# Dealing queued work by cost, with heads' tiles dealt anew and S's split kept on VectorE

## The chip, the cores and the metric

The kernel runs on one core of a Trainium2 chip. The time is device microseconds of one execution, from its first to its last instruction with what lies around them; of several executions the median is given. A core has engines that run side by side and meet through semaphores: TensorE (PE, matmuls), VectorE (DVE), ScalarE (ACT), GpSimd (POOL), and SyncE (SP), which here issues transfers. Each engine works through its own instructions in the order in which the program was written down.

## The reference

One layer of a hybrid decoder is computed for 1024 prompt rows and 8 x 4 sample rows, width 1024, in float32:

```python
z = _rmsnorm(x, norm_mix_g)
p = z @ w_in                      # h, c, b | u, v | q | gate logits gA, gB, gM
...
conv_out, conv_a_state = _causal_dwconv3(a_c * a_h, conv_a_prev, conv_a_w)
y_a = a_b * conv_out
y_b = u * _spatial_gate(v_n, sg_w, sg_b)
y_m = _mem_attention(q, mem_k, mem_v)      # 4 heads of 256, 256 memory rows
g = jax.nn.sigmoid(g.astype(jnp.float32)).astype(x.dtype)
g_a, g_b, g_m = jnp.split(g, N_BRANCH, axis=-1)
x = x + (g_a * y_a + g_b * y_b + g_m * y_m) @ w_o
h = _rmsnorm(x, norm_ffn_g) @ w_up
hc, conv_f_state = _causal_dwconv3(h, conv_f_prev, conv_f_w)
hc = hc + conv_f_b
a, gt = jnp.split(hc, 2, axis=-1)
x = x + (jax.nn.silu(gt) * a) @ w_down
```

The prompt's attention reads one shared memory (256 rows); each of the 8 sample groups has a cached memory of its own. The updated caches are outputs too.

## The kernel before

All activations stand with channels on the partitions and the 1056 rows (T) side by side, in 8 tiles of 128 channels. A float32 product is made of three matmuls on rounded parts: a value is split into a high part (cast on ScalarE) and a low part (value less high part, mostly on VectorE), and `three` (L205 to L207) adds high x high, high x low and low x high. `zhi` and `zlo` hold the parts of the normalised input, later of `S`, the sum of the gated branches.

The stages in order of time: norm and v (to about 240 us), the main stage (244 to 686), the pair stage (691 to 1029), w_o, the up projection, the down projection (to the end).

**Main stage.** It makes u, gB, q and gM, tile by tile (`main`). A tile is 3 chunks of 352 rows, and a chunk is 24 matmuls into one of three PSUM buffers `mm`. A u chunk is evacuated by one VectorE instruction (L1077), a gB chunk by a sigmoid on ScalarE (L1072) and one product on VectorE (L1091), a gM chunk by a sigmoid and two VectorE instructions (L1099, L1100). The order of tiles is the list `plan`, in which `"u0"` means tiles 0 and 1 of u, `"B1"` tiles 2 and 3 of gB, and so on; each string is the work during which one head's attention is done, the first and the last string go without one.

**Queued work.** What the attention and other small steps issue is put as closures into a queue `aux`. Twice in a chunk (after 12 matmuls, and at its end; I call this a slot) `weave` takes items off the queue: `pace(n)` says that the queue is to be empty after n slots, and `weave` gives out the number of items that this asks for. `drain` gives out all that are left. An item is called when its turn comes, and its instructions then stand on every engine behind all that was written before.

**A head's items** (`att_items`): `rows` turns the sample rows' q and writes them to DRAM (L816); `fetch` loads cached keys and values; `fetch_q` loads q rows to all partitions (L825); 16 `product` items, four VectorE products each (L837), make the sample rows' scores, each followed by an item that is a load or nothing; `kv_load` and `kv_split` bring the prompt's keys and values of this head and split them (cast on ScalarE, low part at L955 on VectorE); `score(i)` makes 12 matmuls (L968 to L970) for 256 prompt rows, then a maximum (L973), exponentials (L976), and the normalised probabilities on VectorE (L980, L983); `turn_p(i)` transposes them (L995); `value(i)` multiplies with the values. Then come the sample rows' softmax, `parts` (splits of the cached values, L883 and L884) and `against` (their matmuls, L897).

**Pair stage.** The projections h, c, b and gA go in steps of a seven-product scheme on 2 x 2 blocks. `b_forms(s)` makes block differences of the input ahead of it: `whole` adds high and low part on GpSimd (L1133), `minus` subtracts blocks on VectorE (L1139), `parts` splits (L1145 ScalarE, L1146 VectorE). `b_sums` makes the weight sums on GpSimd (L1191 to L1193), `b_prepare` splits a weight block for one step (L1204 ScalarE, L1205 VectorE). A step's 24 matmuls go to one of three PSUM buffers `pair`, and VectorE or ScalarE evacuates them (L1264 to L1291). These buffers lie where `mm` lay. `ORDER = (1, 2, 6, 5, 7, 3, 4)` is the order of a pair's seven steps.

**End of the pair stage.** In the last pair `b_end` says what follows each step: `to_parts` splits finished tiles of `S` into `zhi` and `zlo` (L1348 ScalarE, L1349 VectorE or GpSimd), `x_back` reads the residual input back into `S`, `units_o` queues the loads of w_o, `split_unit` and `split_lows` split its tiles (L182, L184).

## Time and profile before

| what | value |
| --- | --- |
| median of 3 runs | 1886.79 us (1886.17 to 1886.82) |
| profiled execution | 1886.49 us |
| its span | 1884.8 us |
| mean granted TensorE clock | 0.981 |
| TensorE idle, waiting for keys' low part (L955) | 27.4 us in 3 waits |
| TensorE idle, 684 to 702 us | 7.45 us |
| TensorE idle, 1010 to 1041 us | 7.15 us |

In the views quoted below, a row of waits names the waiting line and what it waited for, then total us, times and longest. A row of the timeline gives start, duration, engine, line, operation, output and inputs, and in brackets the idle time ahead of it with what ended it. A row of windows gives, for each engine, busy time and number of instructions, then the granted clock (1.00 is full speed), the share of the transfer engines and GB/s.

### The profile page before, as it was taken

To read this page: it belongs to the slowest core of one execution; us is meant where nothing else is said; L and a number is where in the kernel's file an instruction comes from. 1 tells how busy PE (TensorE), PEld (TensorE's weight loads), DVE (VectorE), ACT (ScalarE), POOL (GpSimd) and SP (SyncE) were. 2 spreads that over 40 slices of the span, in tenths; PEclk is the share of its full clock that TensorE was granted. 3 is DMA by queue.
4 is the path that set the end of the run, shared out by engine and by line. 5 is a ranking of instruction groups with operands and counts; after the bars stand their busy time and mean duration, and the time that the engine had idled before them with its cause. 6 is when DMAs were issued, how large, how long until landed. Compare 5 with 4: busy or idle time off the path is not lost.

```text
span 1884.8 us, 32215 instructions
## 1 busy us (share of the span) xinstructions
PE 1803.8 (96%) x12960; PEld 1774.1 (94%) x12960; DVE 1303.6 (69%) x2246; ACT 694.2 (37%) x1133; POOL 489.8 (26%) x545
## 2 busy tenths in 40 slices
PE   9999999989897989999998999999999999999997
PEld 8988999989897889999998998899999999899997
DVE  5577665574838687676868578888988898655433
ACT  6654325223332332232233333433333333444332
POOL 2231100000000424233322223566656654100000
PEclk9999999999998989999998999999999999999999
DMA  8736252524334201111113730222222322776652
GB/s 265 209 106 204 78 191 79 164 82 147 105 101 138 70 13 56 46 57 57 46 48 97 203 91 29 85 76 87 79 75 70 92 75 90 227 244 227 201 164 89
DMA packets 250145, 215.11 MB, mean 114 GB/s; under 512 B 7941, under 2 KB 235437, under 8 KB 249997
## 3 DMA queue, kind: packets, MB, share of 16 engines
q1 hardware_dynamic: 243252, 203.81, 35.0%
q10 hardware_dynamic: 6745, 9.25, 1.4%
q8 instruction: 102, 1.67, 0.4%
q14 instruction: 46, 0.38, 0.1%
HBM read 183.22 MB, written 29.81 MB: 113 GB/s over the span
## 4 chain that ended last, share of the span: by engine, by line
PE 57%; DVE 17%; issue 10%; POOL 9%; ACT 3%; DMA 2%; ACTq 0%; SPq 0%; DVEq 0%; POOLq 0%
PE pair L206 11%; PE pair L207 11%; PE pair L205 11%; PE mm L205 5%; PE mm L207 5%; PE mm L206 5%; DVE fs L837 4%; POOL fs L1663 2%; DVE wl L184 2%; POOL S L1575 2%; DVE fs L1646 1%; POOL S L1574 1%; POOL ws L1596 1%; POOL S L1573 1%; DVE wh L1593 1%
## 5 line engine op out<-in xcount | busy, mean ns | idle before, releaser
L205 PE MATMUL pair<-zhi,wh 128*128 128x264 f32 (+1 forms) x1608 | 474.9, 295 | 15.3 <-ACT zhi L1348 6.0
L206 PE MATMUL pair<-zlo,wh 128*128 128x264 f32 (+1 forms) x1608 | 471.6, 293 | 1.9 <-DVE zlo L1349 1.2
L207 PE MATMUL pair<-zhi,wh 128*128 128x264 f32 x1216 | 347.4, 286 | 2.4 <-DVE wh L1205 2.4
L205 PE MATMUL pair<-fs,wh 128*128 128x264 f32 (+1 forms) x1124 | 330.9, 294 | 4.7 <-DVE fs L1687 4.1
L206 PE MATMUL pair<-fs,wh 128*128 128x264 f32 (+1 forms) x1124 | 327.7, 292 | 0.7 <-DVE fs L1460 0.7
L205 PEld LDWEIGHTS pair<-zhi,wh 128*128 128x128 f32 x1608 | 306.9, 191 | 20.0 <-ACT zhi L1348 6.4
L205 PE MATMUL mm<-zhi,wh 128*128 128x352 f32 x960 | 315.4, 329 | 0.3 <-ACT zhi L267 0.3
L206 PE MATMUL mm<-zlo,wh 128*128 128x352 f32 x960 | 312.0, 325 | 1.0 <-POOL zlo L278 1.0
L207 PE MATMUL mm<-zhi,wl 128*128 128x352 f32 x960 | 311.1, 324 | 0.2 <-DVE wl L184 0.2
L206 PEld LDWEIGHTS pair<-zlo,wh 128*128 128x128 f32 x1608 | 307.0, 191 | 2.7 <-DVE zlo L1349 1.5
L184 DVE TENSOR_TENSOR wl<-ws,wh 128x1024 fp32r<-128x1024 f32 (+1 forms) x151 | 187.4, 1243 | 163.4 <-ACT wh L182 162.8
L207 PE MATMUL pair<-fs,wh 128*128 128x264 f32 x904 | 256.2, 283 | 0.0
L207 PEld LDWEIGHTS pair<-zhi,wh 128*128 128x128 f32 x1216 | 231.1, 190 | 2.7 <-DVE wh L1205 2.7
L205 PEld LDWEIGHTS pair<-fs,wh 128*128 128x128 f32 x1124 | 212.1, 189 | 5.8 <-ACT fs L1629 4.0
L206 PEld LDWEIGHTS pair<-fs,wh 128*128 128x128 f32 x1124 | 212.2, 189 | 0.9 <-DVE fs L1460 0.9
L182 ACT CAST wh<-ws 128x1024 fp32r<-128x1024 f32 (+1 forms) x152 | 153.5, 1013 | 150.8 <-PE pair L206 94.3
L206 PEld LDWEIGHTS mm<-zlo,wh 128*128 128x128 f32 x960 | 181.8, 189 | 1.8 <-POOL zlo L278 1.5
L205 PEld LDWEIGHTS mm<-zhi,wh 128*128 128x128 f32 x960 | 182.3, 190 | 1.1 <-ACT zhi L267 0.6
L207 PEld LDWEIGHTS mm<-zhi,wl 128*128 128x128 f32 x960 | 181.8, 189 | 0.5 <-DVE wl L184 0.5
L207 PEld LDWEIGHTS pair<-fs,wh 128*128 128x128 f32 x904 | 170.4, 188 | 0.0
L1646 DVE SCALAR_TENSOR_TENSOR fs<-fs,vec,fs 128x1024 f32<-128x1024 f32 x88 | 132.9, 1510 | 0.0
L207 PE MATMUL pair<-zhi,wl 128*128 128x352 f32 (+1 forms) x392 | 123.9, 316 | 1.4 <-DVE wl L184 1.4
(323 smaller groups left out, 3179.7 us busy)
## 6 DMA issues: line engine op xcount, KB each, us to landing
ws<-in_w_in SPq DMA_DIRECT2D x88, 512.0 KB, 4.5
ws<-in_w_down SPq DMA_DIRECT2D x60, 512.0 KB, 4.6
fs<-q_d SPq DMA_DIRECT2D x32, 512.0 KB, 8.4
ws<-in_w_up SPq DMA_DIRECT2D x46, 256.0 KB, 3.9
act_d<-fs SPq DMA_DIRECT2D x22, 528.0 KB, 3.2
S<-in_w_up SPq DMA_DIRECT2D x42, 256.0 KB, 2.9
fs<-in_cache_mem_k SPq DMA_DIRECT2D x16, 512.0 KB
fs<-in_cache_mem_v SPq DMA_DIRECT2D x16, 512.0 KB, 3.5
```

Source lines behind the costliest of these rows:

```text
L182: nc.scalar.copy(out=hi, in_=t)
L184: lows.append(lambda: eng.tensor_tensor(out=lo, in0=t, in1=f32(hi), op=ALU.subtract))
L205: mmul(ps, lhsT=wh, rhs=xh, start=first, stop=False)
L206: mmul(ps, lhsT=wh, rhs=xl, start=False, stop=False)
L207: mmul(ps, lhsT=wl, rhs=xh, start=False, stop=last)
L837: nc.vector.tensor_tensor_reduce(out=att["qr"][:, :256], in0=q[:, i, :], in1=t[:, 2 * (bb % 2) + mt, :], scale=1.0, scalar=0.0, op0=ALU.mu ...
L1573: tt(out=s1, in0=a21, in1=a22, op=ALU.add)
L1574: tt(out=s2, in0=s1, in1=a11, op=ALU.subtract)
L1575: tt(out=a21, in0=a11, in1=a21, op=ALU.subtract)
L1593: nc.vector.tensor_tensor(out=lo, in0=a, in1=f32(hi), op=ALU.subtract)
L1646: nc.vector.scalar_tensor_tensor(out=o[:, :NP], in0=hb[:, k : k + NP], scalar=w, in1=o[:, :NP], op0=ALU.mult, op1=ALU.add)
L1663: nc.gpsimd.tensor_tensor(out=g[:, :T], in0=g[:, :T], in1=outs[j, 0][:, :T], op=ALU.mult)
```

## The change

It has three parts. Line numbers of the changed kernel are 8 higher from the weaving on (9 and 12 near the end of the pair stage and behind).

1. *Weaving.* Each item of a head has a cost: 2.2 for a product, 0.2 for the item after it, 1.4 for the keys' split, 0.8 for `parts`, 0.4 for the others; items without a cost count 1. `weave` shares out costs and no longer numbers. The plan is dealt anew, so that four heads have 46, 34, 34 and 34 slots (58, 34, 34 and 30 before). Keys' load and split come one group of products sooner.
2. *Forms and sums.* The first half's `b_forms` begin one gB tile earlier and have 12 slots, where they had 6. `b_sums(0)` goes behind three of the second half's forms, where it stood behind all of them, and that queue has 11 slots, where it had 12.
3. *End of the pair stage.* All of S's splits go to VectorE, in pieces of two tiles; `units_o` is called after step 6, where it was after step 2; the last steps are the same in another notation.

```diff
+    def cost(go):
+        return getattr(go, "cost", 1.0)
+
+    def at_cost(x, go):
+
+        go.cost = x
+        return go
+
     def weave():
         split_lows()
-        due[0] += len(aux) / slots_left[0]
+        due[0] += sum(cost(go) for go in aux) / slots_left[0]
         slots_left[0] = max(1, slots_left[0] - 1)
-        while aux and due[0] > 0.999:
-            due[0] -= 1
+        while aux and due[0] > cost(aux[0]) - 0.001:
+            due[0] -= cost(aux[0])
             aux.popleft()()
...
-    for names in ("q0", "u0 B0 u1 B1 q1", "M0 u2 q2", "M1 B2 q3", "M2 u3 B3", "M3"):
+    for names in ("q0", "u0 B0 u1 q1", "B1 M0 q2", "M1 u2 q3", "B2 M2 u3 B3", "M3"):
...
-            no = lambda: None
+            no, small_no = lambda: None, at_cost(0.2, lambda: None)
...
-                    items.append(product(bb, mt))
-                    items.append(fetch_q(bb + 2) if mt and bb + 2 < 8 else no)
+                    items.append(at_cost(2.2, product(bb, mt)))
+                    items.append(at_cost(0.2, fetch_q(bb + 2)) if mt and bb + 2 < 8 else small_no)
...
+                if bb == 4:
+                    items += [kv_load, started]
                 if bb == 5:
-                    items += [kv_load, started]
-                if bb == 6:
-                    items.append(kv_split)
+                    items.append(at_cost(1.4, kv_split))
...
-                items.append(parts(bb // 2, bb % 2))
+                items.append(at_cost(0.8, parts(bb // 2, bb % 2)))
...
-            return items
+            return [go if hasattr(go, "cost") else at_cost(0.4, go) for go in items]
...
-                pace(6 * len(seq) - 2 if h < 3 else 30)
+                pace(6 * len(seq) - 2 if h < 3 else 34)
...
-                if (n, f) == ("gB", 7):
+                if (n, f) == ("gB", 6):
                     drain()
                     aux.extend(b_forms(0))
-                    pace(6)
+                    pace(12)
                 if (n, f) == ("gM", 6):
-                    aux.extend([lambda: (b_load(0, 0), b_load(0, 1), b_load(1, 0))] + b_forms(1))
-                    aux.extend([lambda: b_sums(0)] + [b_prepare] * 4)
-                    pace(12)
+                    forms1 = b_forms(1)
+                    aux.extend([lambda: (b_load(0, 0), b_load(0, 1), b_load(1, 0))] + forms1[:3])
+                    aux.extend([lambda: b_sums(0)] + forms1[3:] + [b_prepare] * 4)
+                    pace(11)
...
-        def to_parts(fr, r, eng=nc.vector):
+        def to_parts(fr, r):
             nc.scalar.copy(out=zhi[:, fr, r], in_=S[:, fr, r])
-            eng.tensor_tensor(out=zlo[:, fr, r], in0=S[:, fr, r], in1=f32(zhi[:, fr, r]), op=ALU.subtract)
+            nc.vector.tensor_tensor(out=zlo[:, fr, r], in0=S[:, fr, r], in1=f32(zhi[:, fr, r]), op=ALU.subtract)
...
         b_end = {
-            1: [lambda: to_parts(slice(0, 4), left, nc.gpsimd)],
-            2: [units_o, lambda: to_parts(slice(4, 6), left, nc.gpsimd)],
-            6: [lambda: to_parts(slice(6, 7), left)],
-            5: [lambda: to_parts(slice(0, 4), right), lambda: x_back(slice(0, 4)), split_unit, split_lows],
-            7: [split_unit, split_lows],
-            3: [lambda: to_parts(slice(4, 6), right), lambda: x_back(slice(4, 6)), lambda: to_parts(slice(7, 8), right)],
+            1: [lambda: to_parts(slice(0, 2), left), lambda: to_parts(slice(2, 4), left)],
+            2: [lambda: to_parts(slice(4, 6), left)],
+            6: [units_o, lambda: to_parts(slice(6, 7), left)],
+            5: [lambda: to_parts(slice(0, 2), right), lambda: to_parts(slice(2, 4), right),
+                lambda: x_back(slice(0, 4)), o_split],
+            7: [o_split],
+            3: [lambda: to_parts(slice(4, 6), right), lambda: x_back(slice(4, 6)), lambda: to_parts(slice(7, 8), right),
+                last_add, lambda: to_parts(slice(6, 7), right)],
         }
```

How this moves instructions is shown at three places on VectorE. The first is head 1 from the keys' low part (L955, now L963) to the first maximum (L973, now L981); a product is a pair of ISA rows (L837, now L845), `sig` and `S` rows are gM evacuations. Before:

```order
L837 ISA fs_3766,sc<-fs_3997,fs_3971 128x256
L837 ISA sc 128x1
L955 TENSOR_TENSOR fs_4081<-fs_4041,fs_4080 128x1024
L837 ISA fs_3766,sc<-fs_4039,fs_3971 128x256
...
L1077 TENSOR_TENSOR S<-mm,S 128x352
...
L973 TENSOR_REDUCE mx_4131<-aux 128x2
L980 RECIPROCAL sm_4132<-sm_4132 128x2
```

Of the change:

```order
L1107 TENSOR_TENSOR sig<-sig,fs_2968 128x352
L1108 TENSOR_TENSOR S<-S,sig 128x352
L963 TENSOR_TENSOR fs_3922<-fs_3861,fs_3921 128x1024
L192 TENSOR_TENSOR wl<-ws,wh 128x1024
L845 ISA fs_3586,sc<-fs_3859,fs_3801 128x256
...
L1107 TENSOR_TENSOR sig<-sig,fs_2969 128x352
L1108 TENSOR_TENSOR S<-S,sig 128x352
...
L845 ISA fs_3586,sc<-fs_3903,fs_3801 128x256
...
L981 TENSOR_REDUCE mx_4031<-aux 128x2
L988 RECIPROCAL sm_4032<-sm_4032 128x2
```

Before, 56 of the 64 products stand ahead of the low part and 8 behind it, with one u evacuation; now 48 and 16, with a weight split and two gM evacuations. On TensorE 264 main matmuls stand between `rows` and the first score of heads 1 to 3 (204, 204 and 180 before), and 276 in head 0 (300 before); after them come two scores, then the first `turn_p` (before, in heads 1 and 2, 12 main matmuls between the two scores).

The second place is VectorE ahead of the first pair step: block differences, splits of them (into `fs`), gM evacuations, and weight splits (`wh`). Before:

```order
L1139 TENSOR_TENSOR fs_6647<-fs_6647,fs_6593 128x1056
L1146 TENSOR_TENSOR fs_6684<-fs_6647,fs_6683 128x1056
L1099 TENSOR_TENSOR sig<-sig,fs_5888 128x352
L1100 TENSOR_TENSOR S<-S,sig 128x352
L1205 TENSOR_TENSOR wh<-ws,wh 128x512 x2
L1099 TENSOR_TENSOR sig<-sig,fs_5888 128x352
L1100 TENSOR_TENSOR S<-S,sig 128x352
L1205 TENSOR_TENSOR wh<-fs_6716,wh 128x512 x2
```

Of the change:

```order
L1147 TENSOR_TENSOR fs_6651<-fs_6651,fs_6593 128x1056
L1154 TENSOR_TENSOR fs_6688<-fs_6651,fs_6687 128x1056
L1213 TENSOR_TENSOR wh<-ws,wh 128x512
L1107 TENSOR_TENSOR sig<-sig,fs_5721 128x352
L1108 TENSOR_TENSOR S<-S,sig 128x352
L1213 TENSOR_TENSOR wh<-ws,wh 128x512
L1213 TENSOR_TENSOR wh<-fs_6595,wh 128x512 x2
L1107 TENSOR_TENSOR sig<-sig,fs_5721 128x352
L1108 TENSOR_TENSOR S<-S,sig 128x352
```

The second half's differences stand at the same gM chunks as before; one weight split has moved ahead of the last-but-one gM evacuation, two more ahead of the last. On GpSimd the three sums stand ahead of the eighth `whole`, where they stood behind it.

The third place is VectorE at the end of the pair stage: weight splits (`wh`), evacuations of `pair`, and splits of `S`. Before:

```order
L1205 TENSOR_TENSOR wh<-ws,wh 128x512 x2
L1267 TENSOR_TENSOR sig<-pair,fs_6771 128x528
L1205 TENSOR_TENSOR wh<-ws,wh 128x512
L1279 TENSOR_TENSOR sig<-sig,fs_9903 128x528
L1280 TENSOR_TENSOR S<-S,sig 128x528
L1289 TENSOR_TENSOR fs_6771<-pair,fs_6771 128x528
L1349 TENSOR_TENSOR zlo<-S,zhi 128x528
L1289 TENSOR_TENSOR fs_6771<-pair,fs_6771 128x528
L1349 TENSOR_TENSOR zlo<-S,zhi 128x4x528
```

Of the change:

```order
L1213 TENSOR_TENSOR wh<-ws,wh 128x512
L1358 TENSOR_TENSOR zlo<-S,zhi 128x2x528 x2
L1213 TENSOR_TENSOR wh<-ws,wh 128x512
L1275 TENSOR_TENSOR sig<-pair,fs_6771 128x528
L1358 TENSOR_TENSOR zlo<-S,zhi 128x2x528
L1213 TENSOR_TENSOR wh<-ws,wh 128x512
L1287 TENSOR_TENSOR sig<-sig,fs_9903 128x528
L1288 TENSOR_TENSOR S<-S,sig 128x528
L1297 TENSOR_TENSOR fs_6771<-pair,fs_6771 128x528
L1358 TENSOR_TENSOR zlo<-S,zhi 128x528
L1297 TENSOR_TENSOR fs_6771<-pair,fs_6771 128x528
L1358 TENSOR_TENSOR zlo<-S,zhi 128x2x528 x2
```

Three splits of two tiles have come in between the weight splits and the evacuations; before they stood on GpSimd, as one of four tiles and one of two.

## The prediction

> **What bounds the kernel now.** The profiled execution took 1886.49 us, 0.3 us below the median of 1886.79; its span is 1884.8 us, so 1.7 us lie around it. The sum is made against 1886.5 and carried to the median as it is. First the page's busy shares:

> ```profile
> PE 1803.8 (96%) x12960; PEld 1774.1 (94%) x12960; DVE 1303.6 (69%) x2246; ACT 694.2 (37%) x1133; POOL 489.8 (26%) x545
> ```

> TensorE is the bound: 81 us of the span idle (1884.8 - 1803.8), and a slow clock in places (the windows below). The change takes no matmul away, so it can win only those. The view of waits, TensorE alone, names them:

> ```profile
> PE aux L969 <- DVE fs L955: 27.4, 3, 11.5
> PE pair L205 <- ACT zhi L1348: 6.0, 2, 3.6
> PE pair L205 <- ACT sig L1072: 5.0, 1, 5.0
> PE pair L207 <- DVE wh L1205: 2.4, 1, 2.4
> PE pair L206 <- DVE zlo L1349: 1.2, 1, 1.2
> PE aux L995 <- DVE fs L983: 1.0, 1, 1.0
> ```

> (Total us, times, longest.) The first row is heads 1 to 3, where the scores wait for the keys' low part, 27.4 us in three waits. The third and fourth stand before the first pair step, the second and fifth at the pair stage's end. Windows over these places (the first two rows are head 1) show what the waits cost besides:

> ```profile
> core 0: us, PE busy (x) PEld busy (x) DVE busy (x) ACT busy (x) POOL busy (x), PEclk, DMA share, GB/s
> 389.90:398.00 8.10, 0.13 (x2) 0.02 (x1) 7.72 (x32) 0.00 (x0) 0.00 (x0) 0.82 0.22 64
> 398.00:402.00 4.00, 4.00 (x17) 4.00 (x18) 3.79 (x18) 0.00 (x0) 0.00 (x0) 0.50 0.00 0
> 684.00:702.00 18.00, 10.55 (x61) 9.95 (x61) 13.65 (x15) 8.29 (x14) 6.63 (x5) 0.72 0.00 0
> 1010.00:1020.00 10.00, 7.23 (x60) 7.01 (x58) 7.77 (x6) 2.13 (x3) 5.27 (x2) 0.99 0.21 56
> 1020.00:1030.00 10.00, 9.17 (x54) 9.20 (x55) 8.30 (x10) 5.03 (x5) 0.00 (x0) 0.67 0.77 250
> 1030.00:1041.00 11.00, 7.45 (x38) 6.94 (x38) 8.54 (x13) 5.00 (x7) 0.00 (x0) 0.69 0.35 114
> ```

> While TensorE is idle VectorE is full (7.72 of 8.10 us), and after each wait the granted clock is 0.50 for some 3.4 us or a multiple, which costs half of that. So a head's wait costs itself and about 1.7 us more: heads 27.4 + 1.0 + 3 x 1.7, say 2 in head 3, about 34 us. Before the pair stage 7.4 us idle and a clock deficit of 0.28 x 18 = 5 us, less what falls in idle time: about 9.7 together. At the pair stage's end 2.8 + 0.8 + 3.6 idle, and about 3 us twice by the clock: 13. That is 57 us at which the change aims.

> **Part 1, heads.** The code's order puts the keys' split after 12 of 16 products, where it stood after 14, and the scores 264 main matmuls (22 slots) behind the head's rows, where heads 1 and 2 had 204 and head 3 had 180. Nothing is added. What VectorE does in head 1 up to the low part, by groups (the first row the products), and the rows that fix the times:

> ```profile
> L837 DVE CUSTOM_DVE_ANT_0 fs<-fs,fs 128x256 f32<-128x256 f32 x56 | 23.7, 423 | 1.6
> L184 DVE TENSOR_TENSOR wl<-ws,wh 128x1024 fp32r<-128x1024 f32 x2 | 2.4, 1220 | 0.0
> L1077 DVE TENSOR_TENSOR S<-mm,S 128x352 f32<-128x352 f32 x2 | 1.0, 518 | 0.0
> 356.83 0.38 PE L816 MATMUL aux<-ident,qs 128*32 128x128 f32 x2
> 364.51 0.42 DVE L837 CUSTOM_DVE_ANT_0 fs<-fs,fs 128x256 f32<-128x256 f32 x1
> 396.70 1.22 DVE L955 TENSOR_TENSOR fs<-fs,fs 128x1024 fp32r<-128x1024 f32 x1
> 401.76 0.69 DVE L973 TENSOR_REDUCE mx<-aux 128x2 f32<-128x512 f32 x1
> 404.54 0.60 PE L995 MATMUL aux<-ident,fs 128*128 128x128 f32 x4
> 675.56 0.52 DVE L1099 TENSOR_TENSOR sig<-sig,fs 128x352 f32<-128x352 f32 x1
> 676.55 2.61 DVE L1139 TENSOR_TENSOR fs<-fs,fs 128x1056 f32<-128x1056 f32 x2
> ```

> Products begin 7.7 us after the rows. From there to 396.70 are 32.2 us; without 4 evacuations of a gM chunk at 0.99 (675.56 to 676.55), 2 weight splits at 1.14 and 2 evacuations at 0.44 (both steps in sequence, a bit under the durations), 25.0 us are left for 56 products, 0.447 each. In the changed order 48 products, 5 + 3 evacuations (gB, gM) and 2 splits stand before the low part of head 1: 21.5 + 2.2 + 3.0 + 2.3 = 29, so it ends at 7.7 + 29 + 1.2 = 37.9 us behind the rows. The scores come at 22 x 1.92 = 42.3 us (a slot is 12 matmuls; a chunk of 24 takes 3.84). So the waits for the keys go, with 4 us to spare.

> What is late next: VectorE's first maximum. Behind the low part stand a split, 16 products and 2 gM evacuations (1.1 + 7.2 + 2.0), so L973 begins at 48.2 us, and the turned probabilities may start 2.8 us later (401.76 to 404.54), at 51.0. TensorE, with two scores of 12 matmuls at about 0.12 us, is there at 45.2. New wait: 5.8 us, less a little where steps overlap; I take 5.5, and the clock's 1.6 with it. Heads 2 and 3 have the same counts within 0.6 us. Head 0 loses 24 main matmuls ahead of its scores (276, not 300): its 1.0 us can grow by at most 3.84; I take 3. After: 3 x 7.1 + 3 = 24, against 34: **-10 us**. Ends: if the new wait is 3 us and head 0 unchanged, -20; if it is 8 us and head 0 pays all, 3 x 10 + 5 = 35, nothing. The middle is nearest to the counted rows.

> The scheduler's own arithmetic is done when the program is built and costs nothing. SyncE's transfers stand in nearly the same order, the keys' load one q load earlier; it was issued at about 375 and used at 396, cover of some 20 us. This cover hides it.

> **Part 2, forms and sums.** Rows before the first pair step:

> ```profile
> 688.38 1.07 ACT L1145 CAST fs<-fs 128x1056 fp32r<-128x1056 f32 x1 [3.18 <-DVE fs L1139]
> 690.74 0.46 ACT L1072 ACTIVATE sig<-mm 128x352 f32<-128x352 f32 x1
> 657.50 4.88 DVE L1139 TENSOR_TENSOR fs<-fs,fs 128x1056 f32<-128x1056 f32 x2
> 690.73 1.58 DVE L1099 TENSOR_TENSOR sig<-sig,fs 128x352 f32<-128x352 f32 x1
> 693.75 1.28 DVE L1205 TENSOR_TENSOR wh<-ws,wh 128x512 fp32r<-128x512 f32 x2
> 688.43 1.27 POOL L1191 TENSOR_TENSOR fs<-ws 128x512 f32<-128x512 f32 x1 [20.88 <-issue]
> 651.10 8.81 POOL L1133 TENSOR_TENSOR fs<-zhi,zlo 128x1056 f32<-128x1056 f32 x3 [8.66 <-ACT sig L1072]
> ```

> The pair's PSUM banks come free with the last sigmoid, 690.74 + 0.46 = 691.2, so the 5.0 us wait began at 686.2, where the main work ended. That sigmoid stands on ScalarE behind a cast that waits for VectorE's difference. VectorE was behind: the gM group of 675.56 belongs to the chunk that ended at 670.8 (four chunks of 3.84 us ahead of 686.2), that of 690.73 to 682.4, 8.3 us late. Part of it came earlier: two differences at 657.50 took 4.88 us instead of 2.6 because GpSimd was adding (651.10 to 659.9). Then the sums on GpSimd from 688.43 stretched a product of 0.52 to 1.58, and the first low part came at 693.75.

> Now the first half's forms are spread over 12 slots from one gB group earlier, sums stand before the last whole block, and one weight split is ahead of the last-but-one gM evacuation. The chain itself (difference 1.25, cast 1.07, difference 1.26, gM 1.0, that is 4.6 us per 3.84 us chunk) stays. Walked through from the gM groups' start without a backlog, it puts the last sigmoid at about 688.1 on the old clock, so 2.0 us of wait stay, and the weights' low part is there before it. 7.4 becomes 2; I leave half of the 2.3 us of clock: **-6.5 us**. Ends: -9.7 (all), and -2 (only the second wait, where the backlog stays because whole blocks again meet VectorE).

> [...]

> ```profile
> 1033.33 0.52 PE L205 MATMUL pair<-zhi,wh 128*128 128x264 f32 x1 [2.38 <-ACT zhi L1348]
> ```

> An idle time of 2.38 us was followed by a clock of 0.69 over 1030 to 1041. [...]

> **Part 3, the pair stage's end.** Six tiles' low parts go from GpSimd to VectorE, in pieces of two:

> ```profile
> 1008.08 4.75 POOL L1349 TENSOR_TENSOR zlo<-S,zhi 128x2112 fp32r<-128x2112 f32 x1 [9.86 <-PE pair L207]
> 1008.55 4.82 DVE L1205 TENSOR_TENSOR wh<-ws,wh 128x512 fp32r<-128x512 f32 x1 [3.28 <-ACT wh L1204]
> 1016.19 2.52 DVE L1205 TENSOR_TENSOR wh<-ws,wh 128x512 fp32r<-128x512 f32 x1 [2.19 <-ACT wh L1204]
> 1019.98 0.70 DVE L1289 TENSOR_TENSOR fs<-pair,fs 128x528 f32<-128x528 f32 x1
> 1006.04 1.96 ACT L1348 CAST zhi<-S 128x2112 fp32r<-128x2112 f32 x1
> 1022.67 2.36 DVE L1349 TENSOR_TENSOR zlo<-S,zhi 128x2112 fp32r<-128x2112 f32 x1 [0.53 <-ACT zhi L1348]
> ```

> A split of 0.64 us (two took 1.28 above) took 4.82 and 2.52 beside GpSimd's subtraction: 6 us lost on VectorE. The same subtraction costs VectorE 2.36 us for four tiles, so six add 3.5. The wait of 3.6 us is put down to ScalarE's cast, but the evacuation of a pair buffer at 1019.98 ended at the same moment, 1020.7, and three buffers are all there are: I take it that TensorE waited from 1017.1 for this one, late behind the 2.52. Placed anew, with ScalarE's cast of two tiles done at 1007.1: two pieces to 1009.5, split 1010.1, evacuation 1010.8 (was 1014.0), piece to 1013.7, split 1014.3, sums 1015.7, and that evacuation at 1016.4, before TensorE needs it at 1017.1. So 3.6 us and the following 3 us of clock go. The later waits, 2.4 and 1.2, hang on the last S tiles, 7 us of VectorE and ScalarE work behind the same evacuations, and stay with their clock loss. w_o's loads are written later, but stand at the same place in SyncE's queue and wait for the same free buffers: nothing. **-6.5 us**. Ends: -13 (all of it), and +3.5, where the added VectorE work is all on the path.

> **The sum**: -10 - 6.5 - 6.5 = -23, 1886.5 - 23 = 1863.5.

> **Rivals.** *B, the wait only moves*: the new wait before the turned probabilities is as long as the old (8 us or more), because products start later than 7.7 us behind the rows or evacuations are denser. For it: VectorE is full there, and its work is not reduced. Against it: counts. -13, 1873. *C, more goes*: probabilities are reached without a backlog (3 us), all of part 2 goes: -20 - 9 - 6.5, 1851. *D, part 3 gives nothing*, VectorE being the longer path with 3.5 us more: 1870. *E, no effect*: waits are conserved because VectorE's work between head and pair stage sets the pace, 1886; against it, VectorE's 69% share. *F, slower*: loads of q (L825) come late, since a head now starts while the last one's values still hold buffers and q loads stand in order on SyncE:

> ```profile
> L825 SPq DMA_DIRECT2D fs<-q_d x32: 319/424/3290, 246.9 to 570.2; - x32
> DMA to landing us min/median/max: 5.2/8.4/10.2
> ```

> The new wait grows one for one with the products' start. To eat 23 us in three heads they must come 7.7 us later, 15.4 us behind the rows; at 18 us the time is 1863.5 + 3 x 10.3 = 1894. Against it: a landing of 10.2 us at most, and heads 1 to 3 stood 552 to 554 TensorE rows apart before too.

> **Chances.** As summed 0.55, B 0.15, C 0.12, D 0.08, E 0.04, F 0.06. The range 1852 to 1877 holds all but E, F and a part of C. A difference of 0.2% (3.8 us) is about what can be told from none: faster 0.90, same 0.04, slower 0.06.

> **What the profile after would show.** Right: no row of scores waiting for the keys' low part; a new row of TensorE waiting for the probabilities (L991, 5 to 6 us, three times); the wait for the last sigmoid near 2 us and none for the first weights' low part; no subtraction of S on GpSimd, splits of 0.7 us near 1010, and 1010 to 1020 full. Wrong: products starting well after 7.7 us, main matmuls waiting for VectorE inside a head, a wait of over 4 us at the first w_o matmuls.

## The result

The changed kernel took 1865.15 us (median of 4 runs, 1864.47 to 1866.39) against 1886.8 us: 0.9886 of the time, with a 95% interval of 0.9869 to 0.9903. It is 21.7 us faster; 1863.5 us was forecast. The profiled execution took 1866.39 us, its span 1864.6.

One sentence of the description above is wrong: the last steps of `b_end` are not the same in another notation. After step 3 the last addition into S stood ahead of all splits, and now stands behind two of them. The run e7 puts it back.

The page's busy shares, and from the view of waits, TensorE alone, the rows that bear on the change (total us, times, longest):

```profile
PE 1802.3 (97%) x12960; PEld 1771.8 (95%) x12960; DVE 1294.5 (69%) x2250; ACT 691.0 (37%) x1133; POOL 480.5 (26%) x543
PE aux L1003 <- DVE fs L991: 15.5, 7, 4.6
PE pair L213 <- ACT zhi L1357: 4.5, 2, 4.0
PE acc L905 <- DVE fs L892: 3.8, 2, 3.6
PE pair L213 <- ACT sig L1080: 1.9, 1, 1.9
PE pair L214 <- DVE zlo L1358: 1.1, 2, 0.9
```

The scores' row, 27.4 us before, is gone. In its place stands the row of the turned probabilities, 15.5 us in seven waits. The wait for the last sigmoid is 1.9 us (5.0 before), that for the first weights' low part is gone, and of the waits at the pair stage's end the one of 3.6 us is gone; 4.0 us at the first w_o matmuls have taken the place of 2.4. One wait has grown: 3.6 us for the split of cached values (L892), where the longest was 2.1 before.

Windows show the stages in one row each. Before, from the first head's rows to the first pair step, and from there to the w_o matmul that waited:

```profile
244.49:691.26 446.77, 407.93 (x2628) 401.68 (x2626) 286.46 (x803) 143.08 (x298) 33.75 (x18) 0.96 0.35 110
691.26:1033.33 342.07, 333.69 (x2701) 332.98 (x2701) 251.47 (x327) 101.23 (x159) 108.30 (x105) 0.98 0.20 58
```

After, between the same matmuls (2628 and 2701 of them again), and the stretch of the first new wait with the one behind it:

```profile
245.33:679.05 433.72, 410.40 (x2628) 404.10 (x2625) 282.95 (x805) 141.22 (x299) 34.39 (x20) 0.97 0.36 113
679.05:1011.30 332.25, 328.29 (x2701) 328.07 (x2701) 243.88 (x328) 100.16 (x159) 98.05 (x101) 1.00 0.20 59
382.00:387.00 5.00, 1.30 (x11) 0.98 (x10) 3.74 (x15) 1.02 (x4) 0.00 (x0) 1.00 0.00 0
387.00:391.00 4.00, 4.00 (x19) 4.00 (x18) 1.58 (x5) 3.20 (x7) 0.00 (x0) 0.57 0.02 4
```

The main stage became 13.0 us shorter, the stretch behind it 9.8 us; 0.8 us were lost ahead of the first head and 1.8 behind, together the 20.2 us between the spans. In the main stage TensorE's idle time fell from 38.8 to 23.3 us, but the same matmuls kept it busy 2.5 us longer: the four waits of 3 to 5 us in the heads were followed by half the clock, as waits of 8 us were before (387 to 391: 0.57, partly at half clock; before, 398 to 402: 0.50).

### The profile page after: what moved, and what is told of

The parts are those of the page before. It is cut to its first block, busy times and chain, and to the rows that moved or that the text cites. A ratio compares the mean times of both kernels' runs of the same rounds, so it can differ in the third digit from the quotient of the medians.

```text
span 1864.6 us, 32222 instructions
## 1 busy us (share of the span) xinstructions
PE 1802.3 (97%) x12960; PEld 1771.8 (95%) x12960; DVE 1294.5 (69%) x2250; ACT 691.0 (37%) x1133; POOL 480.5 (26%) x543
## 5 line engine op out<-in xcount | busy, mean ns | idle before, releaser
L213 PE MATMUL pair<-zhi,wh 128*128 128x264 f32 (+1 forms) x1608 | 473.1, 294 | 11.5 <-ACT zhi L1357 4.5
```

The costliest lines, as they stand in the source:

```text
L213: mmul(ps, lhsT=wh, rhs=xh, start=first, stop=False)
```

## The experiments

Each run is the changed kernel with one edit, except where another is named, and differences in us are against its 1865.15 us. It was not timed again beside them. The kernel before was: 1887.2 us beside e1 to e4, 1887.9 beside e5 to e8, 1887.4 beside e9 to e12, against 1886.8 us in the result. The ratios to that kernel are known to 0.0013 to 0.0017, which is 2.5 to 3 us. The 95% intervals of e1, e2, e5, e7, e8 and e12 overlap that of the changed kernel, and e3's touches it; those of e4, e6, e9, e10 and e11 lie apart.

**e1: part 2 taken back.**

```diff
-                if (n, f) == ("gB", 6):
+                if (n, f) == ("gB", 7):
...
-                    pace(12)
+                    pace(6)
...
-                    aux.extend([lambda: b_sums(0)] + forms1[3:] + [b_prepare] * 4)
-                    pace(11)
+                    aux.extend([lambda: b_sums(0)] + [b_prepare] * 4)     # behind all of b_forms(1)
+                    pace(12)
```

> The changed kernel with part 2 taken back (forms again from the last gB tile with 6 slots, sums again behind all of the second half's forms, 12 slots). By my theory, worked out from the two profiles (TensorE's idle time between the gM tiles and the first pair step 7.45 before, 1.84 after; lost by the slow clock 2.6 before, nothing after), the 8 us of part 2 come back: 1873 us, with a wait of about 5 us for the last sigmoid (L1080) and about 2.4 us for the first weights' low part. Rival: what shortened this stage was the heads' new dealing, which leaves VectorE without a backlog when the gM tiles begin; then the time stays at 1865 to 1867 and both waits stay small.

Measured: 1868.5 us (1866.14 to 1870.67), 3.4 us more. The rival was right on the first wait, and neither on all of it; the time alone is not clear of noise, the waits in the profile are. The waits between 640 and 700 us, and the first two block differences:

```profile
PE pair L215 <- DVE wh L1213: 2.8, 1, 2.8
PE pair L213 <- ACT sig L1080: 1.7, 1, 1.7
647.39 2.62 DVE L1147 TENSOR_TENSOR fs<-fs,fs 128x1056 f32<-128x1056 f32 x2
```

Without part 2 the last sigmoid is still in time (1.7 us, not 5.0), since two differences take 2.62 us, not 4.88: no longer than the two at 676.55 in the kernel before (2.61), where GpSimd was idle. I take it that its whole blocks are done by then. Only the second wait is back; it and the clock behind it (0.50 from 682 to 688 us) are what part 2 is worth.

**e12: in e1, the old plan and the old slots as well**, so that of part 1 only the costs and the sooner split are left.

```diff
-    for names in ("q0", "u0 B0 u1 q1", "B1 M0 q2", "M1 u2 q3", "B2 M2 u3 B3", "M3"):
+    for names in ("q0", "u0 B0 u1 B1 q1", "M0 u2 q2", "M1 B2 q3", "M2 u3 B3", "M3"):
-                pace(6 * len(seq) - 2 if h < 3 else 34)
+                pace(6 * len(seq) - 2 if h < 3 else 30)
```

> The kernel without part 2 (1868.5 us), and in it the old plan of tiles and the old number of slots (58, 34, 34, 30); costs, the sooner split and part 3 stay. Theory: the new plan's worth is that the last head ends well ahead of the forms, so that GpSimd's whole blocks no longer meet the first block differences; with the old plan these take 4.9 us for two again, the last sigmoid comes late (a wait of 4 to 5 us ahead of the pair stage) and head 3 has a longer wait with its 30 slots: 1874 to 1878 us. Rival: giving out by cost is all, and the time stays under 1871.

Measured: 1870.43 us (1869.11 to 1872.74), 1.9 us above e1, with overlapping intervals: the rival. The wait for the last sigmoid is 3.5 us, and head 3 waits 6.4 us, as the theory had it, but head 0 waits only 1.1, and the first two differences take 2.61 us here too: giving out by cost (with the sooner split) is enough to keep GpSimd's blocks off them, which end at 646.57 us, where the differences begin at 648.01.

**e4: items given out by number again, with the new plan.**

```diff
-        return getattr(go, "cost", 1.0)
+        return 1.0
```

> The changed kernel with every item's cost 1, so that items are given out by number again; the new plan, the keys' place and parts 2 and 3 stay. My theory: giving out by cost is what puts the scores 22 slots behind the rows; by number they come after about 18, ahead of the keys' low part (37.9 us behind the rows) and 8 to 10 us ahead of the probabilities. Waits of 8 us and more in all four heads come back, head 0 included since it has only 46 slots now: 1877 us or more. Rival: the new plan and the sooner split do it, the cost little: under 1868.

Measured: 1878.67 us (1877.38 to 1879.56), 13.5 us more. The theory holds, with waits of 5.5 to 8.1 us in a head where it had 8 and more; its two rows of waits:

```profile
PE aux L1003 <- DVE fs L991: 20.5, 4, 6.4
PE aux L977 <- DVE fs L963: 7.8, 3, 3.9
```

In heads 1 to 3 keys' low part and probabilities are both waited for, in head 0 the probabilities alone (5.5 us).

**e3: the keys' load and split one group later, as before.**

```diff
-                if bb == 4:
+                if bb == 5:
                     items += [kv_load, started]
-                if bb == 5:
+                if bb == 6:
                     items.append(at_cost(1.4, kv_split))
```

> The changed kernel with the keys' load and split one group of products later, as before. My theory: the low part then ends at 7.7 + 32.5 + 1.2 = 41.4 us behind the head's rows and the scores come at 42.3, so nothing or under 1 us per head is lost, 1865 to 1868 us; the new wait for the probabilities stays, since the work ahead of the first maximum is the same. Rival: the sooner split is what removed the keys' wait, and without it the wait is back: 3 to 4 us per head and the clock behind it, 1875 or more.

Measured: 1860.83 us (1856.53 to 1861.87), 4.3 us faster, which neither had. As the theory said, no score waits for the keys, though it is close: in heads 1 to 3 the low part ended 42.3 to 42.5 us behind the rows, and the scores began at 42.5. But the second waits for probabilities are gone too. What differs there is ScalarE's loading of the exponential's table ahead of the third score; of the changed kernel first, then of e3:

```profile
392.90 1.28 ACT L984 ACT_TABLE_LOAD   x1 [1.85 <-DVE mx L981]
390.62 1.28 ACT L984 ACT_TABLE_LOAD   x1
```

In the first it waited for VectorE's maximum and came into the chain with its 1.28 us; in the second it was over when the maximum came. The program's order shows why: there the table's load carries a wait for VectorE, and in e3 only waits for transfers; I take it that the buffer which the probabilities were given had last been used on VectorE. In the changed kernel such a load stands between the scores in heads 1 and 3 alone (a gate's sigmoid has come between them), it waits so in both (1.85 and 1.87 us), and only these heads have second waits (1.65 and 0.55 us).

**e10: another buffer there**, no instruction more or less (the buffer that is passed over goes to the end of the list, so tiles dealt later move on by one).

```diff
+                    if i == 2:
+                        for _ in range(1):
+                            fs.put(fs.get())
                     p = fs.get()
```

> The changed kernel, except that the third score's probabilities take the next free buffer in the list; no instruction more or less. In the changed kernel ScalarE's loading of the exponential's table ahead of the third score carries a wait for VectorE in heads 1 and 3, because of the buffer; with the other buffer it carries only waits for transfers. Theory: that wait is why the later split of the keys, which also changed the buffer, was 4 us faster: the second waits for probabilities (1.65 us in head 1, 0.55 in head 3) go, with the clock loss behind the first of them, and the time is 1861 to 1863 us. Rival: the buffer is nothing, the later split itself gains, and the time stays at 1865.

Measured: 1859.75 us (1857.56 to 1861.89), a ratio of 0.9853 (0.9838 to 0.9867) against 0.9886: the theory, with a little more than it asked. The table's load and the row of waits:

```profile
391.00 1.28 ACT L987 ACT_TABLE_LOAD   x1
PE aux L1006 <- DVE fs L994: 12.7, 4, 3.8
```

Four waits are left of seven. So e3's gain was the buffer's, and the sooner split of the keys was worth nothing. Of the 5.4 us the profiles show 2.2 in the second waits and 1.7 in the slow clock behind the first of them (at 397.52 us in the changed kernel); in all the slow clock cost the heads 10.3 us in the changed kernel's profile and 5.1 in e10's, so a part of the gain is clock behind other waits.

**e2: part 3 taken back** (`to_parts` and `b_end` of before).

> The changed kernel with part 3 taken back (the six tiles on GpSimd in one piece of four and one of two, w_o's loads after step 2, the last addition ahead of the last splits). By the two profiles part 3 is worth 1.6 us of idle time and 2.8 us of clock: 1869 to 1870 us, with a wait of 3.6 us behind the fifth step. Rival, the forecast's own size: 6.5 us, 1871.6. Rival on the other side: the end is bound by the last S tiles whatever comes before, so nothing changes, 1865.

Measured: 1867.5 us (1866.85 to 1870.64), 2.4 us more, not clear of noise; the expected 4 to 5 us is not reached. The weight splits and the wait of before are back:

```profile
992.34 4.75 POOL L1358 TENSOR_TENSOR zlo<-S,zhi 128x2112 fp32r<-128x2112 f32 x1 [10.06 <-PE pair L215]
992.81 4.82 DVE L1213 TENSOR_TENSOR wh<-ws,wh 128x512 fp32r<-128x512 f32 x1 [3.48 <-ACT wh L1212]
1000.45 2.52 DVE L1213 TENSOR_TENSOR wh<-ws,wh 128x512 fp32r<-128x512 f32 x1 [2.19 <-ACT wh L1212]
PE pair L213 <- ACT zhi L1357: 5.8, 2, 3.6
```

From the first pair step to the first w_o matmul on a low part (at 1019.28 in e2, 1012.59 in the changed kernel) part 3 brings 6.8 us, but from there to the end e2 needs 849.6 us and the changed kernel 852.0, so 2.4 us are given back. Laid side by side matmul by matmul, the two profiles lose 1.1 us of this in the first 150 matmuls of w_o and 1.6 at about 1600 us, where the slow clock lasts 6.8 us in the changed kernel and 3.4 in e2; a little comes back between. The second loss lies far behind everything that part 3 touches.

**e5: the six tiles on GpSimd again, in the change's pieces.**

```diff
-            1: [lambda: to_parts(slice(0, 2), left), lambda: to_parts(slice(2, 4), left)],
-            2: [lambda: to_parts(slice(4, 6), left)],
+            1: [lambda: to_parts(slice(0, 2), left, nc.gpsimd), lambda: to_parts(slice(2, 4), left, nc.gpsimd)],
+            2: [lambda: to_parts(slice(4, 6), left, nc.gpsimd)],
```

> The changed kernel with the low parts of S's first six left tiles on GpSimd again, but in the change's pieces of two and at the change's places. If part 3 works because GpSimd's subtraction slowed VectorE's weight splits, the splits near 1000 take 2 us and more again, the wait behind the fifth step is back, and the time is that without part 3, 1867 to 1869 us. Rival: the order of the pieces does it, and this kernel stays at 1865. Not told apart by less than 2 us.

Measured: 1865.82 us (1863.78 to 1868.06), as the changed kernel: the medians lie less than the 2 us apart that were asked for. The profile does tell:

```profile
986.58 7.83 POOL L1358 TENSOR_TENSOR zlo<-S,zhi 128x1056 fp32r<-128x1056 f32 x3 [9.09 <-ACT zhi L1357]
988.02 1.58 DVE L1213 TENSOR_TENSOR wh<-ws,wh 128x512 fp32r<-128x512 f32 x1 [3.48 <-ACT wh L1212]
992.42 2.54 DVE L1213 TENSOR_TENSOR wh<-ws,wh 128x512 fp32r<-128x512 f32 x1 [2.20 <-ACT wh L1212]
997.08 0.36 PE L213 MATMUL pair<-zhi,wh 128*128 128x264 f32 x1 [0.54 <-ACT zhi L1357]
```

The splits are still slow beside GpSimd (0.68 alone), yet the first needs 1.58 us, not 4.82, and the wait is 0.54 us, not 3.6. Of the 3.6 us the pieces of two (with w_o's loads called later) take 3.1, the engine 0.5. Here a VectorE split that meets GpSimd's subtraction loses what is left of that one: the two of e2 and the two of e5 each end 0.54 to 0.55 us after the GpSimd instruction beside them (992.81 + 4.82 against 992.34 + 4.75, for one). What it costs is in the rows: 4.82 us beside 4.75 us of GpSimd, 1.58 and 2.54 beside three instructions of 7.83 together. Why the one holds up the other, no run shows.

**e7: the last addition first.**

```diff
-            3: [lambda: to_parts(slice(4, 6), right), lambda: x_back(slice(4, 6)), lambda: to_parts(slice(7, 8), right),
-                last_add, lambda: to_parts(slice(6, 7), right)],
+            3: [last_add, lambda: to_parts(slice(4, 6), right), lambda: x_back(slice(4, 6)),
+                lambda: to_parts(slice(7, 8), right), lambda: to_parts(slice(6, 7), right)],
```

> The changed kernel with the last addition into S ahead of the last splits after step 3, as before, not between them. Theory: the wait of 3.95 us at the first w_o matmuls hangs on the two-tile split, which then stands 1.4 us later on VectorE: up to 1.5 us slower, 1865 to 1867. Rival: it hangs on the tile that the addition makes, and the time falls by 1 to 2 us.

Measured: 1862.31 us (1861.95 to 1862.84), ratio 0.9862 (0.9847 to 0.9876). The intervals overlap, and the place itself shows nothing: from the first pair step to the first w_o low part 333.9 us, against 333.5, and the first wait there is 3.95 us in both. The order is worth nothing there. Of the 3.8 us between the two profiles, 1.5 arise at about 400 us, where a slow clock of 3.4 us in the changed kernel has no counterpart in e7, and 1.4 at about 1600, where it lasts 6.8 against 3.4; both lie where the two programs do the same. Why all four runs of e7 were faster than all four of the changed kernel stays open.

**e6: empty items**, so that TensorE has main work while the probabilities are made. **e8: the same idea on e3.**

```diff
-            items += [score(0), score(1), turn_p(0), score(2), ...
+            gap = lambda x: at_cost(x, lambda: None)
+            items += [gap(3), score(0), score(1), gap(8), turn_p(0), score(2), ...     # e8: gap(5), gap(6)
```

> The changed kernel with empty items of cost 3 ahead of the first score and of cost 8 between the second score and the first turned probabilities, so that about 5 slots of main matmuls stand in the new wait. My theory: the wait stands because TensorE is early, not because VectorE is late for all that follows; then three waits of 3 to 5 us, the second ones and most of the clock's loss at them (15.5 us of idle time and up to 8 us of clock in four heads) go but for some 4 us: 1848 to 1853 us. Rival: VectorE's work of a head sets the pace, the wait moves behind (values, splits of cached values) and the time stays above 1860.

> The kernel with the keys' load and split one group later, and empty items of cost 5 ahead of the first score and 6 ahead of the turned probabilities. Theory as for the gaps of 3 and 8: the scores come at about 41 us behind the rows, the low part at 41.4, the turned probabilities at about 50: 1848 to 1853 us. Rival: as the kernel without gaps, 1861.

Measured: e6 1856.86 us (1854.55 to 1860.88), e8 1865.94 (1863.52 to 1867.42). In e6 no turned probability is waited for, but the first values now wait, twice in heads 1 and 3 (1.8 and 1.7 us, 2.0 and 1.7) and once in head 2 (1.6): the time lies between theory and rival. In e8 both missed, and the gaps cost 5 us against e3: the waits for values are there, and in head 3 TensorE waits 5.4 us for the splits of cached values.

**e9: the gap divided** (6 ahead of `turn_p(0)`, 2 ahead of `value(0)`).

> The kernel with gaps, with the second gap divided: 6 ahead of the turned probabilities, 2 ahead of the first values, which waited for the split of the turned probabilities (1.8 and 1.7 us in heads 1 and 3, 1.6 in head 2). If those waits are only TensorE being early again, some 5 us of idle time go and a little comes back at the turned probabilities: 1852 to 1856 us, against 1856.9 with the gap in one piece. Rival: the wait only moves between the three places, 1857.

Measured: 1853.3 us (1851.03 to 1855.52), 0.9815 (0.9798 to 0.9831) of the time before, as expected, and the fastest of all. The four largest rows of its waits in the heads:

```profile
PE acc L905 <- DVE fs L892: 4.5, 5, 2.1
PE aux L1003 <- DVE fs L991: 3.6, 6, 1.1
PE acc L905 <- ACT fs L891: 2.1, 2, 1.1
PE aux L214 <- DVE fs L1010: 2.1, 2, 1.0
```

**e11: in e9, GpSimd's whole blocks take the buffers freed last.**

```diff
-                    t[n] = fs.get()
+                    t[n] = fs.get_last()
```

> The kernel with the divided gap, and GpSimd's whole blocks take the buffers that were freed last, so that the first of them has to wait for the last head's matmuls with cached values. Theory: GpSimd's additions slow the splits of cached values (0.7 us alone, 2.3 and 2.9 beside them), TensorE waits 3.6 us for those, with 1.7 us of clock behind it; with the additions later both go: 4 us under the divided gap. Rival: the additions are only moved onto the block differences, which then slow down, and the gain is under 1 us.

Measured: 1856.68 us (1855.62 to 1858.22), 3.4 us more than e9. The first half of the theory holds: the splits of cached values take 0.68 us, the wait for them is 1.1 us, and from the first head to the gM tiles no slow clock is left. But the rest is the rival, and more than it had: the additions are late for the differences, and the last sigmoid is waited for longest of all. TensorE's main work ended at 659.65 us, 6.3 sooner than in e9, and the first pair step came at 668.84, 1.0 later.

```profile
PE pair L217 <- ACT sig L1085: 9.2, 1, 9.2
600.67 0.68 DVE L896 TENSOR_TENSOR fs<-fs,fs 128x512 fp32r<-128x512 f32 x1
648.84 2.35 DVE L1152 TENSOR_TENSOR fs<-fs,fs 128x1056 f32<-128x1056 f32 x1
```

## Why the prediction was right, and where its terms were not

The sum (-23) and the time (1863.5) came out within 1.7 us; the split among the parts did not. That the sum is so close is partly luck: by the medians part 1 brought some 6 us more than its term, parts 2 and 3 some 3 and 4 less.

- **Part 1, -10.** Taking back the others leaves 21.7 - 3.4 - 2.4 = 16 us for it, if the parts add up (e1 and e2 are known to about 3 us). Its own working held: the keys' wait is gone, and the wait for the probabilities came where it was said, 3.70, 3.16 and 4.61 us where 5.5 was taken. In heads 1 and 2 most of the difference is the term "products begin 7.7 us after the rows"; besides, the turned probabilities began 2.4 to 2.5 us behind the maximum, where 2.8 was taken:

```profile
337.17 0.38 PE L824 MATMUL aux<-ident,qs 128*32 128x128 f32 x2
343.62 0.43 DVE L845 CUSTOM_DVE_ANT_0 fs<-fs,fs 128x256 f32<-128x256 f32 x1 [2.97 <-DMA fs<-q_d]
372.64 1.22 DVE L963 TENSOR_TENSOR fs<-fs,fs 128x1024 fp32r<-128x1024 f32 x1
384.01 0.69 DVE L981 TENSOR_REDUCE mx<-aux 128x2 f32<-128x512 f32 x1
386.39 0.81 PE L1003 MATMUL aux<-ident,fs 128*128 128x128 f32 x4 [3.70 <-DVE fs L991]
530.29 0.38 PE L824 MATMUL aux<-ident,qs 128*32 128x128 f32 x2
537.95 0.42 DVE L845 CUSTOM_DVE_ANT_0 fs<-fs,fs 128x256 f32<-128x256 f32 x1 [4.18 <-DMA fs<-q_d]
577.97 0.68 DVE L981 TENSOR_REDUCE mx<-aux 128x2 f32<-128x512 f32 x1
```

  In head 1 products began 6.45 us behind the rows, the low part ended at 36.7 (37.9 forecast), the maximum came at 46.8 (48.2); in head 2 6.2 and 46.2; in head 3 7.66 and 47.7, and its wait is the longest. Head 0 waited 1.8 us, where 3 was taken. The clock was sized too low (1.6 us in each of three heads): 10.3 us were lost from the first head to the gM tiles (each window's busy time by its missing clock), against 8.4 before, though the waits were half as long. So from the first head to the gM tiles, 418.5 us became 408.6, the forecast -10, by a shorter wait and a dearer clock that happened to cancel. What part 1 brought besides lay ahead of the pair stage, next point.
- **Part 2, -6.5.** The stretch from the gM tiles to the first evacuated pair step did lose 8 us, and the wait for the sigmoid is 1.85 us where 2 was walked out. But the step "walked through without a backlog" put down to part 2 what part 1 does: e1 has no backlog either. Part 2's own is the second wait with its clock, 3.4 us by the medians. After the remaining 1.85 us the clock was not halved in the changed kernel's profile (nothing lost from 654 to 682 us), nor in e3 to e8 and e10; in e2 and e9 the same wait was followed by 1.7 us of loss. I had left half of the loss; which of the two comes is told by where the wait falls on the clock's grid (last section), and the program doesn't set that.
- **Part 3, -6.5.** The evacuation placed at 1016.4, 0.7 us ahead of TensorE's need, ended 0.7 us ahead of it (at 999.19, the matmul at 999.88), and the 3.6 us wait is gone. At its place 6.8 us are saved (e2), which bears out the term; of this 1.1 are lost in w_o, where "stays with its clock loss" had nothing of it, and 1.6 to the clock at about 1600 us. So the profiles show 5.7 of the 6.5 us, and the medians' 2.4 less than that. But the mechanism was only in part the one named: e5 has the slow splits (1.58 and 2.54 us) and hardly the wait (0.54). The size of the instruction that stands in the way counted, more than its engine.
- **Nothing.** The sooner split was costed at nothing, with 4 us to spare at the scores, and e3 bears out the nothing: without it no score waits, though by 0.2 us at most. But moving items also deals the buffers anew, which put a table load into a chain; that was not thought of (5.4 us, e10).
- **Rivals.** F's case (q late) did not come: products began 6.2 to 7.7 us behind the rows. C's -20 for the heads is about what e9 reaches with gaps: its gM tiles begin at 642.75 us, 20.2 sooner than before, where the changed kernel's begin 9.0 sooner.

## What to carry to other kernels

When queued work is paced, weigh items by the engine that has to do them, and count what stands on that engine ahead of the result that TensorE will wait for next; then put independent matmuls into just that place (e9, 12 us more). A long instruction on an engine that slows the critical one is worth cutting into pieces before it is moved (e5: 3.1 of 3.6 us). And look at which buffer a tile gets: here it decided where a wait stood, and a wait that landed on a table load lengthened a chain by the load (1.28 us).

## What was not expected of the hardware

The clock makes the same program differ by as much as several of the edits under test. Up to the first pair step, the changed kernel, e2, e5 and e7 are one program, with the same waits within 1.0 us each; windows from the first head's rows (of the changed kernel it stands above), e5 and e2:

```profile
245.50:675.60 430.10, 407.41 (x2627) 401.02 (x2625) 283.03 (x805) 141.20 (x299) 34.40 (x20) 0.98 0.36 114
246.66:678.96 432.30, 408.48 (x2629) 402.18 (x2626) 282.54 (x805) 141.20 (x299) 34.39 (x20) 0.98 0.36 114
```

430.1, 432.3 and 433.7 us: TensorE is busy 407.4 to 410.4 us with the same matmuls. From that first row to the gM tiles the slow clock cost 6.8 us in e5 and 10.3 in the changed kernel. Head 2's wait, 3.3 us in e5, was followed by no loss at all there; in the changed kernel 3.2 us were followed by some 6 us at half clock.

```profile
676.64:680.05 3.41, 1.55 (x12) 1.26 (x12) 3.38 (x5) 2.77 (x6) 1.43 (x1) 1.00 0.01 2
680.05:683.46 3.41, 3.41 (x18) 3.41 (x17) 3.27 (x6) 0.00 (x0) 0.10 (x1) 0.50 0.00 0
677.41:680.82 3.41, 1.76 (x14) 1.77 (x15) 3.38 (x6) 2.10 (x5) 1.44 (x1) 1.00 0.01 2
680.82:684.23 3.41, 3.41 (x30) 3.41 (x30) 2.87 (x6) 1.87 (x3) 0.10 (x1) 1.00 0.00 0
```

In e2 the whole wait lies in one window, which is idle for 54.5%, and the next runs at half clock; in the changed kernel a part of it lies ahead, the window is idle for 48%, and the next runs at full clock. Of all windows between 240 and 1030 us in the 14 profiles that began at full clock, the 3040 that were idle for less than 48% were followed by full clock and the 65 with 54.4% or more by half; the 19 between went either way. From these shares I estimate that a wait of under 1.6 us alone costs no clock (0.48 x 3.41), one of over 3.7 us always does (2 x 0.544 x 3.41, for a wait that the grid cuts in halves), and for one between, the grid decides. Where it lies is luck, so the price of a wait of 2 to 3.7 us can't be planned, and a few runs tell edits of 2 or 3 us apart only where the profile shows the wait itself.
